# Hybrid decoder block on one core: rows of x loaded first, small products regrouped in shared breaks, the convolution's chains set apart, fh at another address

## The chip, the cores and the metric

One NeuronCore of a Trainium2 chip runs the whole block in one launch. The metric is device time in microseconds (us), lower is better. A run's time is somewhat longer than the span that the profile shows from the first to the last instruction of one profiled execution.

## The reference, cut to what matters

256 tokens of width 1024, one layer. Everything is float32.

```
n = rmsnorm(x, norm1_g);  z = n @ w_in        # conv u, conv gate, q, k, v, two branch gates
a = u * sigmoid(gate)
y_conv = silu(layernorm(depthwise_conv31(a))) @ w_conv_out
att = attention(rmsnorm(q), rmsnorm(k), v)    # 8 heads of 128, ALiBi, causal; one block of 256
merged = sigmoid(gc) * y_conv + sigmoid(ga) * (att @ w_attn_out)
h = x + merged @ w_out
out = h + (silu(n2 @ w_gate) * (n2 @ w_up)) @ w_down      # n2 = rmsnorm(h, norm2_g), width 2816
```

## The kernel before, in words

**Main products.** Each weight and each activation is split into a high and a low fp32r part, and a product is three matmuls per k-tile: high by high (L141), low activation by high weight (L142), high activation by low weight (L143). The stationary operand is 128 tokens of the activation, the moving one 512 columns of weights. The work is cut into 147 *slots*; a slot is one 512-KB piece of weights (two k-tiles by 512 columns) and issues 12 matmuls: six for token tile 0, six for token tile 1. The slots are, in order: conv (slots 0 to 15), q0 k0 v0 (16 to 27), q1 k1 v1 (28 to 39), g, ao, co, wo, gu and, last, dn, whose activations are the tiles fh and fl. SyncE (SP) streams the raw pieces; ScalarE (ACT) makes `whi` of each (L123), VectorE (DVE) or, for every second piece of slots 12 to 59, GpSimd (POOL) makes `wlo` (L124), six slots ahead.

**The order of the rest.** Four lists of jobs per slot are emitted in program order by the loop at L663 to L696: `pre` ahead of the slot, `jobs` between its two token tiles, `post` behind its second tile, `late` after that. Every engine runs its own queue in that order, so an instruction that waits holds all that stands behind it on its engine. A place in a slot where TensorE (PE) leaves the main matmuls for small ones is called a *break* here.

**Start.** Eight k-rows of x (`xt`, each 256 tokens and one float of gain) come in five DMAs between the first pieces of weights; ACT and DVE split them into `xgh` and `xgl`. POOL adds the squares of x (L631, L633), and in slot 4 PE sums them over the partitions with a column of ones (`ss`, L648).

**Depthwise convolution.** Its 248 taps run on DVE (L219 first tap of a tile, L221 the others), 31 per tile of 128 channels, as two chains: even tiles in PSUM buffer cv0, odd tiles in cv1. When a tile is done, DVE clears the head of its buffer (`clear`, L203), and REFILL slots later PE transposes the next tile into it (`refill`, L209). `run_taps` (L224) deals the taps out over the slots by a planner's costs (SLOT, TAP, LAG) and alternates between the chains. A finished pair of tiles is transposed back for the layer norm (`norm_stats`, L284).

**Heads.** Of each group of four heads, `turn` (L375) transposes q and k (`tq`, read by ACT into qT and kT, L380, L381), `score` (L383, `sc`) multiplies them, DVE adds the bias and takes the maximum (L394), ACT takes the exponentials and divides (L402, L408), `turn_p` (`tp`, L413) transposes, `values` (`pv`, L421) multiplies by v. Their PSUM tiles all come from the tag `tr` with two buffers. The tiles q and k of a group have one buffer each (`scale`, L338): the scaled q of heads 4 to 7 is written over that of heads 0 to 3.

Of the kernel before, what the change touches and what calls it, by code (L numbers as in the profile page):

```python
# [16 lines left out]
P = 128  # L17
# [24 lines left out]
AHEAD = 6  # L42
# slots after which the next heads follow
HEAD_STEP = ((0, 3, 6, 9), (0, 3, 5, 7))
# weights of the work, by which the taps are dealt out over the slots
SLOT = 2.6
# [3 lines left out]
LAG = 1.0  # L50
REFILL = 2
WARM = 8
TABLE_SLOT = 57


class Chunk:
    """CW output columns of one product, for all tokens: nk k-tiles in pieces of G."""

# [6 lines left out]
def hybrid_block(ctx: ExitStack, tc: tile.TileContext, x, xT, par, w_in, w_co, w_ao, w_o, w_gu, w_dn, out):  # L65
# [13 lines left out]

# [1 line left out]
    slots = []  # L81
# [4 lines left out]
    def add(*chunks):  # L86
        """One chunk, or two of which each half is done in turn."""
        n = chunks[0].nk // G
        parts = [range(n)] if len(chunks) == 1 else [range(n // 2), range(n // 2, n)]
        for part in parts:  # L90
            for c in chunks:
                slots.extend((c, g) for g in part)
# [7 lines left out]
    def stream_dma(upto):  # L100
        while at["dma"] < min(upto, len(slots)):
            i = at["dma"]
            c, g = slots[i]
            raw[i] = wp.tile([P, G, CW], F32, tag="raw", bufs=RAW_BUFS, name=f"raw{i}")
            for part in parts(i):
                nc.sync.dma_start(raw[i][:, part, :], c.w[g][:, part, :])
                between(i, part)
            at["dma"] += 1
# [24 lines left out]
    def mm3(c, i, g, t, acc=None, cols=slice(0, CW), first=0, last=None):  # L133
        """Piece g of the chunk for token tile t; the sum runs from k-tile first to last."""
        xh, xl = c.lhs()
        acc = c.acc[t] if acc is None else acc
        last = c.nk - 1 if last is None else last
        tok = slice(t * P, (t + 1) * P)
        for j in range(G):
            k = g * G + j  # L140
            nc.tensor.matmul(acc, xh[:, k, tok], hi[i][:, j, cols], start=(k == first), stop=False)  # L141
            nc.tensor.matmul(acc, xl[:, k, tok], hi[i][:, j, cols], start=False, stop=False)  # L142
            nc.tensor.matmul(acc, xh[:, k, tok], lo[i][:, j, cols], start=False, stop=(k == last))  # L143

# [1 line left out]
    prm = cst.tile([P, N_PAR], F32, name="prm")  # L146
    xt = ea.tile([P, KD, S + 1], F32, tag="vs", name="xt")
    xs = cst.tile([P, T, D], F32, name="xs")

# [1 line left out]
    warm = cst.tile([P, CW], BF16, name="warm")  # L151
    nc.vector.memset(warm, 0.0)
# [5 lines left out]
    load_table(AF.Sigmoid)  # L158
    wps = bank("wps", CW)
    for _ in range(WARM):  # L160
        nc.tensor.matmul(wps, warm[:, :P], warm, start=True, stop=True)
    ident = cst.tile([P, P], F32, name="ident")
    make_identity(nc, ident)
    mhalf = cst.tile([P, 8], F32, name="mhalf")
    nc.gpsimd.memset(mhalf, -0.5)
# [10 lines left out]
    def rsqrt_mean(o, ss, n, width):  # L176
        """o = (ss / n + EPS) ** -0.5"""
        nc.gpsimd.tensor_scalar(o, ss, 1.0 / n, EPS, op0=ALU.mult, op1=ALU.add)
        nc.gpsimd.tensor_tensor(o, o, mhalf[:, :width], op=ALU.pow)

# [1 line left out]
    xg, aoT, yT, mT, hT = {}, {}, {}, {}, {}  # L182
# [7 lines left out]

# [1 line left out]
    cacc, ca = {}, {}  # L192
# [12 lines left out]
    def refill(ch):  # L205
        """The channels of the next tile go on the partitions, after KC - 1 zeros."""
        j, cv = ch["next"], ch["cv"]
        for t in range(T):
            nc.tensor.transpose(cv[:, KC - 1 + t * P : KC - 1 + (t + 1) * P],  # L209
                                ca[j // 2][:, t, (j % 2) * P : (j % 2 + 1) * P], ident)  # L210
        cacc[j] = ea.tile([P, S], F32, tag="cacc", bufs=4, name=f"cacc{j}")
        ch["j"], ch["k"], ch["next"] = j, 0, j + 2
# [11 lines left out]
    def run_taps(slot, until):  # L224
        while load["dve"] + TAP <= until:
            live = [ch for ch in chains if ch["j"] is not None]
            if not live:
                return
            load["turn"] += 1
            ch = live[load["turn"] % len(live)]  # L230
            conv_tap(ch)
            load["dve"] += TAP if len(live) > 1 else TAP_ALONE
            if ch["k"] == KC:
                j, ch["j"] = ch["j"], None
                want_refill(slot, ch)
                if j % 2:
                    last = j == KD - 1
                    at_ = slot + 3
                    while not last and busy[at_] > 1:
                        at_ += 1  # L240
                    busy[at_] += 1
                    jobs[at_].append(lambda p=j // 2: norm_stats(p))
                    pe_side[at_] += 0.45
                    dve_side[at_] += 0.7
                    if last:
                        for i in range(4):
                            (post if i % 2 else jobs)[at_ + 2 + i // 2].append(lambda i=i: norm_back(2 * i))

    def want_refill(slot, ch):
        j = ch["next"]  # L250
        if j < KD and j // 2 in ca:
            clear(ch)
            slot += REFILL
            post[slot].append(lambda: refill(ch))
            pe_side[slot] += 0.25
            dve_side[slot] += 0.1
# [58 lines left out]

# [1 line left out]
    vs = {}  # L317
# [36 lines left out]
    def v_done(b):  # L354
        def done(slot, acc):
# [5 lines left out]
            late[slot + 1].append(lambda: evac(0))  # L361
            late[slot + 2].append(lambda: evac(1))
            for i in range(4):
                head(slot + 1 + i, slot + 2 + HEAD_STEP[b][i], 4 * b + i)
        return done

    def head(first, slot, h):
        hs = slice((h % 4) * P, (h % 4 + 1) * P)
# [14 lines left out]
        def score():  # L383
            s["bias"] = sm.tile([P, 3, P], F32, tag="bias", name=f"bias{h}")
            nc.scalar.mul(s["bias"], dist, 2.0 ** (-8.0 * (h + 1) / H))
            s["sc"] = bank(f"sc{h}", 4, P)
            nc.tensor.matmul(s["sc"][:, 0, :], s["q"][:, :P], s["k"][:, :P], start=True, stop=True)
            nc.tensor.matmul(s["sc"][:, 1:3, :], s["q"][:, P:], s["k"], start=True, stop=True)
            most()
# [35 lines left out]

        for i in (first, slot, slot + 4, slot + 5):
            busy[i] += 1
        pe_side[first] += 0.45
        pe_side[slot] += 0.65
        pe_side[slot + 4] += 0.35  # L430
        pe_side[slot + 5] += 0.65
        dve_side[slot] += 0.7
        dve_side[slot + 5] += 0.35
        jobs[first].append(turn)
        jobs[slot].append(score)
        pre[slot + 2].append(expo)
        pre[slot + 3].append(divide)
        jobs[slot + 4].append(turn_p)
        jobs[slot + 5].append(values)

# [1 line left out]
    sgs = ea.tile([P, 2, T, D], F32, tag="sgs", name="sgs")  # L442
# [21 lines left out]

# [1 line left out]
    def merge_done(b):  # L466
# [26 lines left out]

# [1 line left out]
    s2 = sm.tile([P, T, 2], F32, bufs=1, name="s2")  # L495

# [37 lines left out]

# [1 line left out]
    ff = {}  # L536
# [42 lines left out]

# [1 line left out]
    for p in range(KD // 2):  # L581
# [18 lines left out]

# [1 line left out]
    xg[0] = pair("xg")  # L602

    def load_x(k0, k1):
        nc.sync.dma_start(xt[:, k0:k1, :], xT[:, k0:k1, :])

    def between(i, part):
        if i == 0:
            load_x(part.start, part.stop)
            if part.stop == G:  # L610
# [4 lines left out]
    def split_x(k):  # L615
        g = xt[:, k, S:]
        nc.scalar.activation(xg[0][0][:, k, :], xt[:, k, :S], AF.Copy, scale=g)
        nc.vector.scalar_tensor_tensor(xg[0][1][:, k, :], xt[:, k, :S], g, xg[0][0][:, k, :].bitcast(F32),
                                       op0=ALU.mult, op1=ALU.subtract)
# [4 lines left out]
    def square(q):  # L624
        """Squares of x, summed over the parts of its rows that share a partition."""
        if q == 0:
            nc.scalar.activation(sq, xt[:, :2, :S], AF.Square)
            return
        s = sm.tile([P, 2, S], F32, tag="u", name=f"xsq{q}")
        nc.scalar.activation(s, xt[:, 2 * q : 2 * q + 2, :S], AF.Square)  # L630
        nc.gpsimd.tensor_add(sq, sq, s)  # L631
# [3 lines left out]
    for i in range(6):  # L635
# [4 lines left out]
        if i >= 2:  # L640
            square(i - 2)
    ones = cst.tile([P, 1], F32, name="ones")
    nc.gpsimd.memset(ones, 1.0)

    def first_norm():
# [12 lines left out]

# [1 line left out]
    n = len(slots)  # L660
# [85 lines left out]
```

## Time and profile before

| what | value |
|---|---|
| median of 3 runs | 446.02 us (445.62 to 446.30) |
| span of the profiled execution, first to last instruction | 443.5 us |
| median less span | 2.5 us |
| PE busy | 437.6 us, 99% |
| DVE, ACT, POOL busy | 309.6, 243.9, 87.5 us |
| clock granted to PE | full in all 40 slices |

No time is given for the profiled execution itself beside its span; the 2.5 us between span and median lie ahead of the first and behind the last instruction. A row of a timeline has the start, the length, the engine, the line, the operation with output and inputs, how many instructions follow each other, and in brackets the engine's idle time before it with what ended it. Matmuls overlap: what one costs on PE is the distance to the next start, not its length.

### The profile page before, as it was taken

What the parts mean: (1) busy time and instruction counts of PE and PEld (TensorE: products, weight loads), DVE (VectorE), ACT (ScalarE), POOL (GpSimd) and SP (SyncE); (2) the same over time, 40 slices, a digit from 0 to 9 for tenths busy, and PEclk for the clock granted to TensorE, in tenths of its full rate; (3) what the DMA queues carried; (4) which work ended last, traced back from release to release, by engine and by line L of the source; (5) the groups of instructions that cost most, each with busy time, mean ns of one, the idle gap of its engine ahead of it and who ended that gap; (6) DMA issues with size and microseconds to landing.
All of it is one profiled execution on the core that took longest, in us unless ns stands there. A gap on an engine that the chain in (4) does not pass through costs nothing.

```text
span 443.5 us, 5743 instructions
## 1 busy us (share of the span) xinstructions
PE 437.6 (99%) x2026; PEld 359.6 (81%) x2026; DVE 309.6 (70%) x523; ACT 243.9 (55%) x439; POOL 87.5 (20%) x73
## 2 busy tenths in 40 slices
PE   8999999999999999999999999999999999999997
PEld 4788888888888888888888888888888888888886
DVE  5989999898899799967586575555555555644501
ACT  6854466689998676639325374444444444633200
POOL 1614465745462443100000000000000000000000
PEclk9999999999999999999999999999999999999999
DMA  8986684355345444544837337655555555585001
GB/s 274 345 271 213 211 303 150 144 185 197 142 149 185 142 137 150 190 163 161 293 95 247 133 120 253 196 189 184 184 185 179 187 181 184 184 252 204 25 0 49
DMA packets 23340, 80.21 MB, mean 181 GB/s; under 512 B 2576, under 2 KB 3216, under 8 KB 23312
## 3 DMA queue, kind: packets, MB, share of 16 engines
q1 hardware_dynamic: 22896, 78.66, 52.9%
q10 hardware_dynamic: 416, 1.19, 0.8%
q8 instruction: 16, 0.26, 0.3%
q14 instruction: 12, 0.10, 0.1%
HBM read 78.79 MB, written 1.05 MB: 180 GB/s over the span
## 4 chain that ended last, share of the span: by engine, by line
PE 94%; POOL 2%; ACT 2%; DMA 1%; SPq 0%; issue 0%; DVE 0%
PE gu L141 9%; PE gu L143 9%; PE gu L142 9%; PE dn L141 4%; PE dn L143 4%; PE dn L142 4%; PE g L143 3%; PE g L142 3%; PE g L141 3%; PE conv L141 2%; PE conv L143 2%; PE conv L142 2%; PE k L143 2%; PE v L143 2%; PE q L143 2%; PE q L141 2%
## 5 line engine op out<-in xcount | busy, mean ns | idle before, releaser
L124 DVE TENSOR_TENSOR wlo<-raw,whi 128x1024 fp32r<-128x1024 f32 (+1 forms) x125 | 153.0, 1256 | 30.5 <-ACT whi L123 29.6
L123 ACT CAST whi<-raw 128x1024 fp32r<-128x1024 f32 (+1 forms) x149 | 148.9, 1035 | 34.9 <-PE dn L142 19.8
L221 DVE SCALAR_TENSOR_TENSOR cacc<-cv,prm,cacc 128x256 f32<-128x256 f32 x240 | 97.2, 475 | 0.2
L141 PE MATMUL gu<-whi,hh 128*128 128x512 f32 x176 | 69.6, 395 | 0.0
L124 POOL TENSOR_TENSOR wlo<-raw,whi 128x1024 fp32r<-128x1024 f32 x24 | 58.1, 2426 | 54.5 <-ACT whi L123 49.6
L143 PE MATMUL gu<-wlo,hh 128*128 128x512 f32 x176 | 68.7, 390 | 0.0
L142 PE MATMUL gu<-whi,hl 128*128 128x512 f32 x176 | 68.5, 389 | 0.0
L143 PEld LDWEIGHTS gu<-wlo,hh 128*128 128x128 f32 x176 | 33.0, 188 | 7.1
L142 PEld LDWEIGHTS gu<-whi,hl 128*128 128x128 f32 x176 | 33.1, 188 | 6.6
L141 PEld LDWEIGHTS gu<-whi,hh 128*128 128x128 f32 x176 | 33.1, 188 | 6.4
L141 PE MATMUL dn<-whi,fh 128*128 128x512 f32 x82 | 32.5, 396 | 0.0
L143 PE MATMUL dn<-wlo,fh 128*128 128x512 f32 x82 | 32.4, 396 | 0.0
L142 PE MATMUL dn<-whi,fl 128*128 128x512 f32 x82 | 32.4, 396 | 0.0
L546 ACT ACTIVATE fs<-gu,rstd 128x256 f32<-128x256 f32 x22 | 10.4, 475 | 39.1 <-PE gu L143 39.1
L548 DVE SCALAR_TENSOR_TENSOR f<-gu,rstd,fs 128x256 f32<-128x256 f32 x22 | 10.6, 484 | 29.1 <-ACT fs L546 29.1
L141 PE MATMUL conv<-whi,xgh 128*128 128x512 f32 x64 | 26.1, 409 | 0.9 <-ACT whi L123 0.8
L141 PE MATMUL g<-whi,xgh 128*128 128x512 f32 x64 | 26.6, 415 | 0.0
L142 PE MATMUL conv<-whi,xgl 128*128 128x512 f32 x64 | 25.4, 398 | 0.0
L143 PE MATMUL conv<-wlo,xgh 128*128 128x512 f32 x64 | 25.4, 397 | 0.0
L143 PE MATMUL g<-wlo,xgh 128*128 128x512 f32 x64 | 25.2, 394 | 0.0
L142 PE MATMUL g<-whi,xgl 128*128 128x512 f32 x64 | 25.0, 391 | 0.0
L561 ACT CAST fh<-ftr 128x512 fp32r<-128x512 f32 x11 | 6.5, 587 | 23.9 <-PE ftr L560 23.9
(159 smaller groups left out, 746.4 us busy)
## 6 DMA issues: line engine op xcount, KB each, us to landing
raw<-in_w_in SPq DMA_DIRECT2D x53, 512.0 KB, 4.2
raw<-in_w_gu SPq DMA_DIRECT2D x44, 512.0 KB, 4.3
raw<-in_w_dn SPq DMA_DIRECT2D x22, 512.0 KB, 4.1
raw<-in_w_ao SPq DMA_DIRECT2D x8, 512.0 KB, 3.3
raw<-in_w_co SPq DMA_DIRECT2D x8, 512.0 KB, 3.3
raw<-in_w_o SPq DMA_DIRECT2D x8, 512.0 KB, 5.1
raw<-in_w_in SPq DMA_DIRECT2D x6, 256.0 KB, 4.7
xs<-in_x ACTq DMA_DIRECT2D x1, 1024.0 KB, 4.7
```

Source lines behind the costliest of these rows:

```text
L123: nc.scalar.copy(hi[i][:, part, :], r[:, part, :])
L124: eng.tensor_sub(lo[i][:, part, :], r[:, part, :], hi[i][:, part, :].bitcast(F32))
L141: nc.tensor.matmul(acc, xh[:, k, tok], hi[i][:, j, cols], start=(k == first), stop=False)
L142: nc.tensor.matmul(acc, xl[:, k, tok], hi[i][:, j, cols], start=False, stop=False)
L143: nc.tensor.matmul(acc, xh[:, k, tok], lo[i][:, j, cols], start=False, stop=(k == last))
L221: nc.vector.scalar_tensor_tensor(cacc[j], src, w, cacc[j], op0=ALU.mult, op1=ALU.add)
L546: nc.scalar.activation(sg, acc[t][:, :256], AF.Silu, scale=r)
L548: nc.vector.scalar_tensor_tensor(f[t], acc[t][:, 256:], r, sg, op0=ALU.mult, op1=ALU.mult)
L561: nc.scalar.copy(fh[:, k2, :], tr)
```

## The change

The gains move to 16 floats in front of x in `xt`, so that each row of x is 256 floats long and starts at an even place; a part of x is issued to the DMA queue ahead of the piece of weights that needs it. The warming matmuls use a 128-wide tile, and there are seven of them. The column of ones is set earlier on POOL. Both groups of heads follow each other at the distances 0, 3, 6, 9 slots; a head's `turn` goes to the slot of the head before's `score`, its `values` to the slot of the head after's `turn_p`, so that two small products share a break. REFILL is 1; a refill goes between the token tiles when that place has a break already; the even chain gets two of three taps until it leads the odd one by 12 taps, after which each chain is refilled at a time of its own; `norm_stats` joins the odd chain's refill where it can. `s2` is padded to 32 floats; it lies ahead of the tiles fh and fl in SBUF, and fh moves from byte 175136 to 174464 of a partition, fl from 197664 to 196992 (before, 32 bytes past a multiple of 64; after, on one). Comments are dropped; line numbers of the changed kernel differ by 5 to 19.

```diff
--- before.py
+++ after.py
@@ -40,21 +40,24 @@
 AHEAD = 6
-HEAD_STEP = ((0, 3, 6, 9), (0, 3, 5, 7))
+HEAD_STEP = (0, 3, 6, 9)
 SLOT = 2.6
...
 LAG = 1.0
-REFILL = 2
-WARM = 8
+REFILL = 1
+LEAD = 12
+WARM = 7
+XG = 16
 TABLE_SLOT = 57
@@ -103,6 +106,8 @@
             for part in parts(i):
+                if i == 0:
+                    load_x(part.start, part.stop)
                 nc.sync.dma_start(raw[i][:, part, :], c.w[g][:, part, :])
@@ -142,13 +147,13 @@
     prm = cst.tile([P, N_PAR], F32, name="prm")
-    xt = ea.tile([P, KD, S + 1], F32, tag="vs", name="xt")
+    xt = ea.tile([P, XG + KD * S], F32, tag="vs", name="xt")
     xs = cst.tile([P, T, D], F32, name="xs")
 
-    warm = cst.tile([P, CW], BF16, name="warm")
+    warm = cst.tile([P, P], BF16, name="warm")
     nc.vector.memset(warm, 0.0)
@@ -156,11 +161,13 @@
     load_table(AF.Sigmoid)
-    wps = bank("wps", CW)
+    wps = bank("wps", 4, P)
     for _ in range(WARM):
-        nc.tensor.matmul(wps, warm[:, :P], warm, start=True, stop=True)
+        nc.tensor.matmul(wps, warm, warm[:, None, :].to_broadcast([P, 4, P]), start=True, stop=True)
     ident = cst.tile([P, P], F32, name="ident")
     make_identity(nc, ident)
+    ones = cst.tile([P, 1], F32, name="ones")
+    nc.gpsimd.memset(ones, 1.0)
     mhalf = cst.tile([P, 8], F32, name="mhalf")
@@ -228,6 +235,11 @@
             ch = live[load["turn"] % len(live)]
+            if len(live) > 1 and load["turn"] % 3 == 0:
+                a, b = chains
+                lead = (a["j"] - b["j"] + 1) // 2 * KC + a["k"] - b["k"]
+                aim = 0 if a["j"] == KD - 2 else LEAD
+                ch = a if lead < aim else b if lead > aim else ch
             conv_tap(ch)
@@ -236,22 +248,24 @@
                     at_ = slot + 3
+                    if not last and not busy[slot + REFILL]:
+                        at_ = slot + REFILL
                     while not last and busy[at_] > 1:
                         at_ += 1
-                    busy[at_] += 1
-                    jobs[at_].append(lambda p=j // 2: norm_stats(p))
+                    (post if at_ == slot + REFILL else jobs)[at_].append(lambda p=j // 2: norm_stats(p))
+                    busy[at_] += at_ != slot + REFILL
                     pe_side[at_] += 0.45
...
                         for i in range(4):
-                            (post if i % 2 else jobs)[at_ + 2 + i // 2].append(lambda i=i: norm_back(2 * i))
+                            jobs[at_ + 2 + i // 2].append(lambda i=i: norm_back(2 * i))
 
...
             slot += REFILL
-            post[slot].append(lambda: refill(ch))
+            (jobs if busy[slot] else post)[slot].append(lambda: refill(ch))
             pe_side[slot] += 0.25
@@ -360,11 +374,15 @@
             late[slot + 2].append(lambda: evac(1))
+            at_ = [slot + 2 + i for i in HEAD_STEP]
             for i in range(4):
-                head(slot + 1 + i, slot + 2 + HEAD_STEP[b][i], 4 * b + i)
-        return done
-    def head(first, slot, h):
+                head(at_[i - 1] if i else slot + 1, at_[i], at_[i + 1] + 4 if i < 3 else at_[i] + 5, 4 * b + i)
+        return done
+    def head(first, slot, end, h):
         hs = slice((h % 4) * P, (h % 4 + 1) * P)
@@ -384,8 +402,8 @@
             s["sc"] = bank(f"sc{h}", 4, P)
+            nc.tensor.matmul(s["sc"][:, 1:3, :], s["q"][:, P:], s["k"], start=True, stop=True)
             nc.tensor.matmul(s["sc"][:, 0, :], s["q"][:, :P], s["k"][:, :P], start=True, stop=True)
-            nc.tensor.matmul(s["sc"][:, 1:3, :], s["q"][:, P:], s["k"], start=True, stop=True)
             most()
@@ -423,22 +441,22 @@
 
-        for i in (first, slot, slot + 4, slot + 5):
+        for i in (first, slot, slot + 4, end):
             busy[i] += 1
...
         pe_side[slot + 4] += 0.35
-        pe_side[slot + 5] += 0.65
+        pe_side[end] += 0.65
         dve_side[slot] += 0.7
-        dve_side[slot + 5] += 0.35
+        dve_side[end] += 0.35
+        jobs[slot].insert(0, score)
         jobs[first].append(turn)
-        jobs[slot].append(score)
         pre[slot + 2].append(expo)
...
         jobs[slot + 4].append(turn_p)
-        jobs[slot + 5].append(values)
+        jobs[end].append(values)
     sgs = ea.tile([P, 2, T, D], F32, tag="sgs", name="sgs")
@@ -491,8 +509,8 @@
 
-    s2 = sm.tile([P, T, 2], F32, bufs=1, name="s2")
+    s2 = sm.tile([P, 32], F32, bufs=1, name="s2")[:, : 2 * T].rearrange("p (t b) -> p t b", b=2)
 
@@ -598,36 +616,39 @@
 
+    def xk(k0, k1):
+        return xt[:, XG + k0 * S : XG + k1 * S].rearrange("p (k s) -> p k s", s=S)
     def load_x(k0, k1):
-        nc.sync.dma_start(xt[:, k0:k1, :], xT[:, k0:k1, :])
+        cols = slice(XG + k0 * S if k0 else 0, XG + k1 * S)
+        nc.sync.dma_start(xt[:, cols], xT[:, cols])
 
...
         if i == 0:
-            load_x(part.start, part.stop)
             if part.stop == G:
...
     def split_x(k):
-        g = xt[:, k, S:]
-        nc.scalar.activation(xg[0][0][:, k, :], xt[:, k, :S], AF.Copy, scale=g)
-        nc.vector.scalar_tensor_tensor(xg[0][1][:, k, :], xt[:, k, :S], g, xg[0][0][:, k, :].bitcast(F32),
+        g, one = xt[:, k : k + 1], slice(k, k + 1)
+        nc.scalar.activation(xg[0][0][:, one, :], xk(k, k + 1), AF.Copy, scale=g)
+        nc.vector.scalar_tensor_tensor(xg[0][1][:, one, :], xk(k, k + 1), g, xg[0][0][:, one, :].bitcast(F32),
                                        op0=ALU.mult, op1=ALU.subtract)
...
         if q == 0:
-            nc.scalar.activation(sq, xt[:, :2, :S], AF.Square)
+            nc.scalar.activation(sq, xk(0, 2), AF.Square)
             return
         s = sm.tile([P, 2, S], F32, tag="u", name=f"xsq{q}")
-        nc.scalar.activation(s, xt[:, 2 * q : 2 * q + 2, :S], AF.Square)
+        nc.scalar.activation(s, xk(2 * q, 2 * q + 2), AF.Square)
         nc.gpsimd.tensor_add(sq, sq, s)
@@ -639,9 +660,6 @@
             square(i - 2)
-    ones = cst.tile([P, 1], F32, name="ones")
-    nc.gpsimd.memset(ones, 1.0)
     def first_norm():
@@ -723,7 +741,8 @@
         "x": x,
-        "xT": np.concatenate([x.T, i["norm1_g"].reshape(D, 1)], axis=1).reshape(KD, P, S + 1).transpose(1, 0, 2),
+        "xT": np.concatenate([vec(i["norm1_g"]), np.zeros((P, XG - KD), np.float32),
+                              x.T.reshape(KD, P, S).transpose(1, 0, 2).reshape(P, KD * S)], axis=1),
         "par": par,
...
         "w_co": cols(i["w_conv_out"][0]),
```

**DVE, the first tile of the even chain (slots 17 to 19).** Here `cacc_368` and `cacc_371` are the first tiles of the even and odd chain in the kernel before, `cacc_367` and `cacc_370` in the changed one; `cv_...` are the PSUM buffers that are cleared. Before:

```order
L221 SCALAR_TENSOR_TENSOR cacc_371<-cv_316,prm,cacc_371 128x256 [waits DVE_49]
L221 SCALAR_TENSOR_TENSOR cacc_368<-cv_314,prm,cacc_368 128x256 [waits DVE_49]
L221 SCALAR_TENSOR_TENSOR cacc_371<-cv_316,prm,cacc_371 128x256 [waits DVE_49]
L203 MEMSET cv_683 128x30 [waits DVE_49]
L221 SCALAR_TENSOR_TENSOR cacc_368<-cv_314,prm,cacc_368 128x256
L203 MEMSET cv_686 128x30 [waits DVE_49]
L124 TENSOR_TENSOR wlo_726<-raw_600,whi_725 128x1024 [waits DMAHW4_49,PE_49,Activation_49]
L219 TENSOR_SCALAR cacc_737<-cv_683,prm 128x256 [waits PE_49]
```

Now:

```order
L228 SCALAR_TENSOR_TENSOR cacc_367<-cv_313,prm,cacc_367 128x256 [waits DVE_49]
L228 SCALAR_TENSOR_TENSOR cacc_370<-cv_315,prm,cacc_370 128x256 [waits DVE_49]
L228 SCALAR_TENSOR_TENSOR cacc_367<-cv_313,prm,cacc_367 128x256 [waits DVE_49]
L210 MEMSET cv_635 128x30 [waits DVE_49]
L228 SCALAR_TENSOR_TENSOR cacc_370<-cv_315,prm,cacc_370 128x256
L228 SCALAR_TENSOR_TENSOR cacc_370<-cv_315,prm,cacc_370 128x256 [waits DVE_49] x2
L226 TENSOR_SCALAR cacc_660<-cv_635,prm 128x256 [waits PE_49]
L228 SCALAR_TENSOR_TENSOR cacc_370<-cv_315,prm,cacc_370 128x256 [waits DVE_49]
```

The first clear moves from behind the 61st tap to behind the 50th, and taps of one chain now stand next to each other (the `x2` row; nine such neighbours ahead of this clear).

**PE, the first refill.** Before, both chains are refilled between the slots 21 and 22 (k). Now the even one is refilled between the slots 18 and 19 (q), the first row of the piece being the last matmul of slot 18. Before:

```order
L143 MATMUL k_1_689<-wlo_603,xgh 128x512
L209 MATMUL cv_683<-ident,ca_387 128x128 [waits DVE_49]
L209 MATMUL cv_683<-ident,ca_387 128x128
L209 MATMUL cv_686<-ident,ca_387 128x128 [waits DVE_49]
L209 MATMUL cv_686<-ident,ca_387 128x128
L141 MATMUL k_0_688<-whi_623,xgh 128x512 [waits Activation_49]
L142 MATMUL k_0_688<-whi_623,xgl 128x512
```

Now:

```order
L147 MATMUL q_1_592<-whi_521,xgl 128x512
L148 MATMUL q_1_592<-wlo_522,xgh 128x512
L216 MATMUL cv_635<-ident,ca_386 128x128 [waits DVE_49]
L216 MATMUL cv_635<-ident,ca_386 128x128
L146 MATMUL q_0_591<-whi_546,xgh 128x512 [waits Activation_49]
L147 MATMUL q_0_591<-whi_546,xgl 128x512
```

The refill of the even chain moves three slots forward on PE, that of the odd one goes behind slot 22.

**ACT, the slots 34 to 36.** `q_1220` (`q_1233` before) is the scaled q of heads 4 to 7, `tq_1254` the transposed q and k of head 3. Before:

```order
L285 COPY yt<-ytr_1219 128x2x256 [waits PE_49]
L344 ACTIVATE q_1233<-q_0_951,m 128x128 [waits Pool_49]
L344 ACTIVATE q_1233<-q_0_951,m 128x128 x3
L408 ACTIVATE p_1195<-p_1195,den_1196 128x128 [waits Pool_49]
L408 ACTIVATE p_1195<-p_1195,den_1196 128x256 [waits Activation_49]
L344 ACTIVATE q_1233<-q_1_952,m 128x128 x4
L123 CAST whi_1255<-raw_1036 128x1024 [waits DMAHW2_49]
L385 ACTIVATE bias_1259<-dist 128x384
L123 CAST whi_1289<-raw_1073 128x1024 [waits DMAHW3_49]
```

Now:

```order
L358 ACTIVATE q_1220<-q_0_953,m 128x128 [waits PE_49,Pool_49]
L358 ACTIVATE q_1220<-q_0_953,m 128x128 x3
L426 ACTIVATE p_1186<-p_1186,den_1187 128x128 [waits Pool_49]
L426 ACTIVATE p_1186<-p_1186,den_1187 128x256 [waits Activation_49]
L358 ACTIVATE q_1220<-q_1_954,m 128x128 x4
L128 CAST whi_1242<-raw_1039 128x1024 [waits DMAHW2_49]
L403 ACTIVATE bias_1246<-dist 128x384
L398 ACTIVATE qT_1259<-tq_1254,gqs 128x256 [waits PE_49]
L399 ACTIVATE kT_1260<-tq_1254,prm 128x256
```

The first scaling of q has a new wait on PE, and head 3's qT and kT stand behind it.

**PE, the middles of the slots 35 and 36.** Now, in slot 35:

```order
L405 MATMUL sc_1248<-kT_1118,qT_1117 128x256 [waits Activation_49]
L406 MATMUL sc_1248<-kT_1118,qT_1117 128x128
L395 MATMUL tq_1254<-ident,q_791 128x128 [waits DVE_49,Activation_49]
L395 MATMUL tq_1254<-ident,q_791 128x128
L395 MATMUL tq_1254<-ident,k_916 128x128 x2
```

and twelve main matmuls later, in slot 36:

```order
L148 MATMUL v_0_1276<-wlo_1072,xgh 128x512
L439 MATMUL pv_1292<-pT_1156,vs 128x256 [waits PE_49,Activation_49]
L440 MATMUL pv_1292<-pT_1156,vs 128x128
L431 MATMUL tp_1297<-ident,p_1186 128x128 [waits DVE_49]
L431 MATMUL tp_1297<-ident,p_1186 128x128 x2
```

The wait on PE in ACT's rows above is for the transposes of `q_791`, the q of heads 0 to 3; the wait of `pv` on ACT is for `kT_1260`, the last reader of `tq_1254`, whose PSUM buffer `pv` takes; that of `tp` on DVE is for the maximum over `sc_1248`. Before, head 3's `turn` stood in slot 31, and `sc` alone in the break of slot 35.

## Rows read from the trace of the kernel before

**Rows 1.** The page: busy time of each engine, its share of the span, instructions.

```profile
PE 437.6 (99%) x2026; PEld 359.6 (81%) x2026; DVE 309.6 (70%) x523; ACT 243.9 (55%) x439; POOL 87.5 (20%) x73
```

**Rows 2.** Windows: each engine's busy time and count, PEclk, DMA share, GB/s.

```profile
50.00:70.00 20.00, 20.00 (x92) 16.56 (x91) 19.46 (x43) 10.57 (x25) 10.65 (x8) 1.00 0.77 266
```

**Rows 3.** Timeline of PE in dn, whose start-to-start distances are even between them.

```profile
400.10 0.40 PE L141 MATMUL dn<-whi,fh 128*128 128x512 f32 x1
...
403.60 0.40 PE L141 MATMUL dn<-whi,fh 128*128 128x512 f32 x1
```

**Rows 4.** Timeline of PE in gu, a stretch without a break.

```profile
330.02 0.39 PE L142 MATMUL gu<-whi,hl 128*128 128x512 f32 x1
...
333.19 0.39 PE L141 MATMUL gu<-whi,hh 128*128 128x512 f32 x1
```

**Rows 5.** The page's costliest groups: the matmuls of dn, first line of three.

```profile
L141 PE MATMUL dn<-whi,fh 128*128 128x512 f32 x82 | 32.5, 396 | 0.0
```

**Rows 6.** Timeline of PE around one break (the refill of both chains).

```profile
69.30 0.60 PE L209 MATMUL cv<-ident,ca 128*128 128x128 f32 x4
69.66 0.48 PE L141 MATMUL k<-whi,xgh 128*128 128x512 f32 x1
69.97 0.40 PE L142 MATMUL k<-whi,xgl 128*128 128x512 f32 x1
```

**Rows 7.** Timeline of POOL at the start: the sums of squares.

```profile
20.32 1.60 POOL L633 TENSOR_TENSOR sq<-sq 128x256 f32<-128x256 f32 x1
21.87 0.09 POOL L643 MEMSET ones<- 128x1 f32 x1
```

**Rows 8.** Timeline of PE around the sum over the partitions.

```profile
21.09 0.39 PE L143 MATMUL conv<-wlo,xgh 128*128 128x512 f32 x1
22.01 0.61 PE L648 MATMUL ss<-ones,sq 128*128 128x1 f32 x4 [0.53 <-POOL ones L643]
```

**Rows 9.** Timeline of DVE ahead of the first refill.

```profile
60.74 4.00 DVE L221 SCALAR_TENSOR_TENSOR cacc<-cv,prm,cacc 128x256 f32<-128x256 f32 x10
64.66 1.21 DVE L124 TENSOR_TENSOR wlo<-raw,whi 128x1024 fp32r<-128x1024 f32 x1
65.80 2.17 DVE L221 SCALAR_TENSOR_TENSOR cacc<-cv,prm,cacc 128x256 f32<-128x256 f32 x5
67.53 0.61 DVE L203 MEMSET cv<- 128x30 f32 x2
```

**Rows 10.** Timeline of PE: the first matmul of slot 19.

```profile
61.14 0.39 PE L141 MATMUL q<-whi,xgh 128*128 128x512 f32 x1
```

**Rows 11.** Timeline of ACT from the first scaling of q on (slots 34, 35).

```profile
110.14 1.15 ACT L344 ACTIVATE q<-q,m 128x128 f32<-128x128 f32 x4
...
113.77 0.59 ACT L385 ACTIVATE bias<-dist 128x384 f32<-128x384 f32 x1
114.20 1.10 ACT L123 CAST whi<-raw 128x1024 fp32r<-128x1024 f32 x1
```

**Rows 12.** Groups by line: kT on ACT (busy, mean ns, idle before).

```profile
L381 ACT ACTIVATE kT<-tq,prm 128x256 f32<-128x256 f32 x8 | 3.7, 467 | 0.0
```

**Rows 13.** Timeline of PE around `sc` in the middle of slot 35.

```profile
112.21 0.38 PE L387 MATMUL sc<-kT,qT 128*128 128x128 f32 x2
...
112.68 0.58 PE L141 MATMUL k<-whi,xgh 128*128 128x512 f32 x1
```

**Rows 14.** Timeline of PE: one head's `turn`.

```profile
98.19 0.38 PE L377 MATMUL tq<-ident,q 128*128 128x128 f32 x2
98.41 0.38 PE L377 MATMUL tq<-ident,k 128*128 128x128 f32 x2
98.55 0.47 PE L141 MATMUL q<-whi,xgh 128*128 128x512 f32 x1
```

**Rows 15.** Timeline of PE in the first slot.

```profile
7.95 0.63 PE L142 MATMUL conv<-whi,xgl 128*128 128x512 f32 x1
8.38 0.63 PE L143 MATMUL conv<-wlo,xgh 128*128 128x512 f32 x1
```

## The prediction, made before the changed kernel had run

> **What bounds the kernel now.** I read the page first: PE is busy for 99% of the span [rows 1], so the time is what PE's queue takes, and the change can gain only where PE spends less per product or has fewer stops, and lose only where PE stops. PE has stops before 22 us alone: waits for the first loads, and one for POOL's sum. Next the windows: from 50 to 70 us DVE is busy 19.46 of 20.00 us beside a full PE [rows 2], so there DVE has no room, and whatever makes PE wait for DVE costs time; ACT with 10.57 us has room on average, which says nothing of its order. Then I compared distances between main matmuls in two stretches without breaks: in dn 15 distances take 3.50 us, 0.2333 each [rows 3]; in gu 14 take 3.17 us, 0.2264 [rows 4]. Last I looked at DVE, ACT and PE around the places where the order moves.
>
> **Gains, each worked out.**
> *fh at another address.* dn has 82 matmuls on each of three lines [rows 5], 246 in all, with the same shapes as gu. The visible difference of dn's operands is that fh and fl start 32 bytes past a multiple of 64. If that is the cause, dn comes to 0.2264, and 246 x 0.0069 = 1.7 us go; the 36 half-wide ones at the end add about 0.1. Bounds: 0 (address has no part) and 1.8. I take 1.8, since no other difference shows.
> *Shared breaks.* PE leaves the main products 45 instead of 52 times; all small matmuls remain. Four transposes cost 0.36 to the next start, and the matmul behind them 0.31 instead of 0.226 [rows 4, 6]: a break costs some 0.04 beyond its own products when the slow matmul is shared. 7 x 0.04 = 0.3 us, bounds 0.1 and 0.7 (all of the 0.08 and a little of what follows).
> *Start.* The sum over the partitions begins at 22.01, when POOL has written the sum (20.32 + 1.60) and then the ones [rows 7, 8]; PE's last main matmul had begun at 21.09. Earlier x shortens PE's waits ahead of this place, but POOL's sum comes no earlier unless ACT's squares do; so what PE gains there it waits again. The ones set earlier give 0.1. Bounds 0 and 1.0. Even addresses of x: nothing, ACT and DVE are not late in what they split there, and at the start only the landings count.
> The padding of s2, the wider moving operand of the warming and the order of the halves of `sc` cost nothing: they lie in idle time or keep the same columns.
> Gains together: 1.8 + 0.3 + 0.1 = 2.2 us.
>
> **Costs, each worked out.**
> *First refill of the even chain.* It now stands ahead of slot 19 and waits for a clear that follows the 50th tap. Before, ten taps start at 60.74, 0.392 apart, and then, behind a low part, five, the last of them behind the first clear [rows 9]; that is, the ten are numbers 48 to 57, and the 50th starts at 61.53 and ends at 62.0. A clear takes 0.3: 62.3. PE reaches slot 19 at 61.14 [rows 10]. That alone is 1.2 us. In the new order nine neighbours ahead of it are of one chain. The row that has such a dependence is the clear at 67.53 behind the tap that starts at 65.80 + 3 x 0.392 = 66.98: 0.55 instead of 0.39 [rows 9]. That includes a change of operation, so I take 0.1 per neighbour, bounds 0 and 0.16: 0.9 us (0 to 1.4). DVE and PE have the same work ahead of this place as before, apart from that. Cost 2.1 (1.2 to 2.6).
> *Refill of the odd chain*, ahead of slot 23. From clear to clear DVE has 23 taps (9.0), two low parts of at least 1.2 [rows 9], three neighbours (0.3) and a clear (0.3): 12.0. PE has four slots of 12 x 0.2264 = 2.72 and one refill (0.2): 11.1. Cost 0.9 (0.4 to 1.6, since low parts that meet POOL's take longer).
> *Third and fourth refill*, ahead of the slots 31 and 35: by the same sum the third has room, the fourth lacks 0.4 (0 to 1.0).
> *Head 3's turn in slot 35.* The first scaling of q for heads 4 to 7 now waits on PE for it. `sc` begins at 112.21 and takes 0.47 [rows 13], `turn` another 0.36 [rows 14]; so ACT starts the scaling at about 113.0, not at 110.14 [rows 11], when its last q transpose has been written, and PE goes on at 113.05. Ahead of kT3 stand eight scalings, two divisions, a high part and a bias: 114.20 - 110.14 = 4.06 [rows 11]; then qT and kT, 0.4 to 0.47 each [rows 12]: 4.9 us. PE has twelve main matmuls, 2.72, and a recovery of 0.1 until `pv`, which waits for kT3. Cost 4.9 - 2.8 = 2.1 (1.5 to 2.6). All of it comes onto PE, whenever PE arrives there, since ACT's chain starts with PE's own transposes.
> *Last refill*, middle of slot 44: 15 taps with seven neighbours, one low part and others since the clear before, some 9 us against two slots and breaks of PE, some 7; what DVE made up during the stop in slot 36 covers most. Cost 0.7 (0 to 1.8).
> Other new waits (`tp`, `tq` of later heads, `norm_back`) have 0.6 us or more of room, worked out in the same way.
> Costs together: 2.1 + 0.9 + 0.4 + 2.1 + 0.7 = 6.2 us.
>
> **Sum.** 443.5 - 2.2 + 6.2 = 447.5 us of span; with the 2.5 us around it, which the change doesn't touch, 450.0 us. The sum goes from one profiled execution to the median of the runs by that difference.
>
> **Rivals.**
> *The stops don't come (faster).* Both groups of stops hang on a few handovers: if DVE's clear comes before 61.1 us and ACT drains in time for `pv`, PE never stops, and 2.2 us of gain stay: 443.8 us. For it: DVE's lag behind PE is set by what PE and POOL hand it, and gaps that a trace of one order shows need not be there in another. Against it: 62.3 against 61.14, and 4.9 against 2.8, are not close. It decides in favour if DVE's backlog at slot 18 is under 2 us and kT3 ready within 2.8 us of the turn.
> *dn stays at 0.2333.* Then the padding has done nothing and 1.8 us are missing: 451.8 us. For it: no row of before shows one product at both addresses. The Trainium skill, page "TensorE: Matmul & The Clock Gate", section on where the extra 2.5 ns come from, gives the distance of back-to-back matmuls by columns and clock alone, 215.7 ns for 512 columns, so by it dn and gu would be alike and no address would matter. The trace disagrees: neither 0.2264 nor 0.2333 is that, and two equal shapes differ by 3%, so something that the rule lacks is at work.
> *The neighbours of one chain are free.* Then the first refill costs 1.2, the second 0.6, the fourth and the last 0.1 and 0.4; with 2.1 for slot 36 that is 4.4: 448.2 us. It is inside my forecast's own range.
> *The clock falls in a stop.* In the first slot matmuls are 0.43 apart [rows 15] against 0.226 later; PE had worked with long waits until then. A stop of 2.1 us with others around it might bring that spacing back for some 4 us: eight matmuls at 0.2 more, 1.7 us: 451.7. Against it: the stop of 0.5 to 0.9 us at 21 to 22 us [rows 8] left 0.23 behind it. The same page of the Trainium skill, in its table of the two states, has an idle engine fall back to half clock; no run here shows a stop long enough.
> *x first brings the sum of squares forward by 1.0 us*: 449.0.
>
> **How the numbers follow.** A run of this kernel can tell 0.2%, 0.9 us, from no change. My forecast with both versions of the neighbours and the earlier sum, 447.5 to 451: 0.68, all slower. dn unchanged or a fallen clock: 0.10, slower. No stops at all: 0.12, faster. Half of the stops, sum near zero: 0.10, no change (445.1 to 446.9). So faster 0.12, same 0.10, slower 0.78. The range leaves out the stop-free case and the dearest: 445.5 to 452.0. Likeliest, 450.0.
>
> **What would show it.** Right: PE waits of about 2 us for the clear ahead of slot 19 and for ACT's kT ahead of `pv` near 118 us, smaller ones ahead of the slots 23 and 44; ACT idle for about 3 us ahead of the first scaling of q; dn at 0.226 to 0.227. Wrong: no wait of PE behind 22 us, or a wait of DVE for PE at the refill; dn still at 0.2333; spacings of 0.43 behind a stop.

## The result, and the profile after

| | before | changed |
|---|---|---|
| median of 4 runs each, side by side | 446.16 us | 450.78 us |
| span of the profiled execution | 443.5 us | 448.4 us |

The change is slower: ratio 1.0107, 95% interval 1.0086 to 1.0128. The forecast was 450.0 us. The page of the changed kernel, against [rows 1], has PE's work unchanged and a longer span:

```profile
span 448.4 us, 5734 instructions
PE 437.7 (98%) x2025; PEld 360.2 (80%) x2025; DVE 310.5 (69%) x523; ACT 244.7 (55%) x439; POOL 88.5 (20%) x73
```

Its waits of PE (engine, line, releaser: total, times, longest) name two that the kernel before did not have, `pv` and `cv`; the third, at the start, was 0.53 us there [rows 8]:

```profile
PE pv L439 <- ACT kT L399: 2.1, 1, 2.1
PE cv L216 <- DVE cv L210: 1.8, 2, 1.3
PE ss L666 <- POOL sq L654: 1.3, 1, 1.3
```

The timeline of PE shows what each stop costs, as the distance from the start of the last main matmul to the start of the product that waited, less the usual 0.227: 1.47 us ahead of slot 19, 0.67 ahead of slot 23, 2.28 in slot 36.

```profile
61.30 0.39 PE L148 MATMUL q<-wlo,xgh 128*128 128x512 f32 x1
62.99 0.44 PE L216 MATMUL cv<-ident,ca 128*128 128x128 f32 x2 [1.31 <-DVE cv L210]
...
73.95 0.39 PE L148 MATMUL k<-wlo,xgh 128*128 128x512 f32 x1
74.85 0.44 PE L216 MATMUL cv<-ident,ca 128*128 128x128 f32 x2 [0.51 <-DVE cv L210]
...
114.72 0.47 PE L146 MATMUL k<-whi,xgh 128*128 128x512 f32 x1
...
117.34 0.39 PE L148 MATMUL v<-wlo,xgh 128*128 128x512 f32 x1
119.85 0.70 PE L439 MATMUL pv<-pT,vs 128*128 128x256 f32 x2 [2.13 <-ACT kT L399]
```

Together these are 4.42 of the 4.9 us that the span grew. The start added 0.36 (slot 5 begins at 22.84, before at 22.48), a short wait at the last refill some 0.3, and dn gave back 0.24.

ACT in slots 35 and 36 is the chain of [rows 11] put behind PE. It sits idle until the transposes of q are done, then needs 4.95 us to the end of kT (114.85 to 119.80):

```profile
114.85 1.14 ACT L358 ACTIVATE q<-q,m 128x128 f32<-128x128 f32 x4 [1.73 <-PE tq L395]
115.86 0.81 ACT L426 ACTIVATE p<-p,den 128x128 f32<-128x128 f32 x2
116.56 1.16 ACT L358 ACTIVATE q<-q,m 128x128 f32<-128x128 f32 x4
117.56 1.09 ACT L128 CAST whi<-raw 128x1024 fp32r<-128x1024 f32 x1
118.49 0.58 ACT L403 ACTIVATE bias<-dist 128x384 f32<-128x384 f32 x1
118.92 0.52 ACT L398 ACTIVATE qT<-tq,gqs 128x256 f32<-128x256 f32 x1
119.27 0.53 ACT L399 ACTIVATE kT<-tq,prm 128x256 f32<-128x256 f32 x1
```

In dn 14 distances take 3.25 us, 0.232 each. In [rows 3] it is 0.2333, and the forecast was 0.2264:

```profile
402.82 0.39 PE L148 MATMUL dn<-wlo,fh 128*128 128x512 f32 x1
...
406.07 0.39 PE L147 MATMUL dn<-whi,fl 128*128 128x512 f32 x1
```

### The profile page after: what moved, and what is told of

It reads as the page before. It is cut to its first block, busy times and chain, and to the rows that moved or that the text cites. A ratio compares the mean times of both kernels' runs of the same rounds, so it can differ in the third digit from the quotient of the medians.

```text
span 448.4 us, 5734 instructions
## 1 busy us (share of the span) xinstructions
PE 437.7 (98%) x2025; PEld 360.2 (80%) x2025; DVE 310.5 (69%) x523; ACT 244.7 (55%) x439; POOL 88.5 (20%) x73
## 4 chain that ended last, share of the span: by engine, by line
PE 79%; DVE 13%; ACT 2%; DMA 2%; issue 1%; SPq 1%; POOL 0%; DVEq 0%; ACTq 0%
PE gu L148 9%; PE gu L146 9%; PE gu L147 9%; DVE cacc L228 8%; DVE wlo L129 4%; PE dn L146 4%; PE dn L148 4%; PE dn L147 4%; PE g L148 3%; PE g L146 3%; PE g L147 3%; PE ao L148 2%; PE ao L146 2%; PE wo L148 2%; PE co L148 2%; PE wo L146 2%
## 5 line engine op out<-in xcount | busy, mean ns | idle before, releaser
L228 DVE SCALAR_TENSOR_TENSOR cacc<-cv,prm,cacc 128x256 f32<-128x256 f32 x240 | 100.1, 475 | 1.3
L129 POOL TENSOR_TENSOR wlo<-raw,whi 128x1024 fp32r<-128x1024 f32 x24 | 59.8, 2495 | 56.7 <-ACT whi L128 56.7
```

The costliest lines, as they stand in the source:

```text
L129: eng.tensor_sub(lo[i][:, part, :], r[:, part, :], hi[i][:, part, :].bitcast(F32))
L228: nc.vector.scalar_tensor_tensor(cacc[j], src, w, cacc[j], op0=ALU.mult, op1=ALU.add)
```

## The experiments

### The two handovers, undone one at a time and together

`e1`: head 3's turn goes back to slot 31.

```diff
-                head(at_[i - 1] if i else slot + 1, at_[i], ...
+                head(slot + 4 if (b, i) == (0, 3) else at_[i - 1] if i else slot + 1, at_[i], ...
```

> The changed kernel with one thing undone: the turn of head 3 goes back from slot 35 to slot 31. Theory (a handover through the one buffer of q): ACT no longer waits for PE ahead of the scaling of q, the stop of 2.3 us ahead of pv in slot 36 goes, and the time falls from 450.8 by about 2.3, to 448.5 us; the stops ahead of the two refills stay as they are. Rival (DVE is late there anyway): the stop only changes its name, to a wait of tp or pv for DVE's maximum, and the time falls by less than 1 us.

Measured: 448.63 us, ratio to before 1.0053 (1.0034 to 1.0072). The wait for kT is gone. A smaller one, which the long stop had covered, stands in its place, so part of the rival holds too: `tp` waits for DVE's maximum, 1.12 us from the start of the last `pv` product. In the changed kernel, where the long stop came first, that distance is 0.11, so the wait costs 1.0.

```profile
118.77 0.38 PE L440 MATMUL pv<-pT,vs 128*128 128x128 f32 x2
120.00 0.52 PE L431 MATMUL tp<-ident,p 128*128 128x128 f32 x3 [0.85 <-DVE nmx L412]
```

By the traces the stops shrink by 2.28 - 1.0 = 1.3 us, and from slot 5 to the end the profiled execution is 1.6 us shorter (423.9 against 425.5). By the medians the time falls by 2.15, and the two intervals allow all of these.

`e2`: the chains as before.

```diff
-REFILL = 1
+REFILL = 2
-            if len(live) > 1 and load["turn"] % 3 == 0:
...
-                ch = a if lead < aim else b if lead > aim else ch
...
-                    if not last and not busy[slot + REFILL]:
-                        at_ = slot + REFILL
...
-            (jobs if busy[slot] else post)[slot].append(lambda: refill(ch))
+            post[slot].append(lambda: refill(ch))
```

> The changed kernel with the chains as before (alternating taps, both refilled together two slots later); heads, start and padding stay changed. Theory (only the new place of the refill makes PE wait): the stops of 1.5 and 0.7 us ahead of the slots 19 and 23 go with their recoveries, 2.3 us in all: 448.5 us, with the stop ahead of pv still there. Rival (DVE is the bound in these slots): the stops come back at the old places of the refills, and the time stays above 450 us.

Measured: 449.65 us, ratio 1.0072 (1.0048 to 1.0096), with runs from 447.4 to 451.7. No `cv` wait is left in the trace and the one for kT stays, as the theory has it; the median is 1.2 us above it. The spread of the ten executions goes with TensorE's granted clock: the three at 1.00 took 447.4 to 448.0 us, the three at 0.995 to 0.996 took 449.1 to 449.7, and the four at 0.992 took 450.6 to 451.7. So at full clock the time is below the theory's 448.5, and the median is raised by the executions with a lower one. The profiled execution (450.55 us, 0.992) shows two falls. The first follows the wait for POOL's sum at the start; in the window behind it (the last three figures are PEclk, DMA share, GB/s) the granted clock is 0.61 on average, and matmuls are 0.43 apart.

```profile
PE ss L659 <- POOL sq L647: 1.4, 1, 1.4
22.00:26.00 4.00, 3.90 (x13) 3.15 (x14) 3.47 (x4) 0.20 (x1) 0.50 (x2) 0.61 0.77 199
```

The second follows the stop in slot 36. There the granted clock is 0.60 and 0.54, and matmuls are 0.42 apart:

```profile
118.00:120.00 2.00, 1.64 (x6) 1.46 (x6) 2.00 (x8) 1.24 (x2) 0.68 (x1) 0.60 0.29 82
120.00:122.00 2.00, 2.00 (x7) 1.67 (x7) 2.00 (x7) 1.70 (x8) 1.70 (x1) 0.54 0.47 180
122.00:124.00 2.00, 2.00 (x11) 1.63 (x10) 2.00 (x6) 2.00 (x9) 0.50 (x1) 1.00 0.62 186
```

```profile
118.36 1.20 PE L432 MATMUL pv<-pT,vs 128*128 128x256 f32 x2 [2.09 <-ACT kT L392]
...
120.86 0.63 PE L147 MATMUL v<-whi,xgl 128*128 128x512 f32 x1
121.28 0.63 PE L148 MATMUL v<-wlo,xgh 128*128 128x512 f32 x1
```

So PE fell from 2.4 to 1.2 GHz after it had stood for 1.4 us, and again after 2.1 us. In the changed kernel's own profiled execution stops of 1.3 and 2.1 us, the waits of `ss` and `pv` above, left the next matmuls at 0.23. Whether a stop of this size is followed by the lower clock differs between executions; what decides it is not shown.

`e12`: both edits.

> Both things undone at once. Theory (independent handovers): 450.8 - 2.3 - 2.3 = 446.2 us, what is left against the kernel before being the later start (+0.4) and dn (-0.2). Rival (the stops cover for each other): one of them comes back elsewhere, 447.5 us or more.

Measured: 446.71 us, ratio 1.0005 (0.9987 to 1.0023): no different from before. Neither stop comes back elsewhere, and the `tp` wait of e1 is gone too. Behind the start one short wait is left that the kernel before did not have, that of the last `norm_stats` for DVE's last tap:

```profile
PE ytr L291 <- DVE cacc L228: 0.4, 1, 0.4
```

### The start alone

The edits to `xt`, `load_x`, `ones`, `warm` on the kernel before.

> The kernel before with the start of the change alone (layout of x, x ahead of the weights, ones earlier, warming). Theory (more waits of ACT for loads make the sum of squares later): PE's sum over the partitions starts about 0.4 us later than before, 22.4 us, and the time is 446.5 us. Rival (the later landings of the changed kernel's profile were chance): the sum is at 22.0 us or earlier, and the time 446.0 us or less.

Measured: 445.87 us, ratio 0.9989 (0.9973 to 1.0005). In its profile the sum did start late, at 22.65, as the theory has it, but the time did not move, as the rival has it. In the profiles of the three kernels below whose start is that of before and whose s2 alone is padded, POOL's sum ended at 22.18, 22.43 and 22.54; before, at 21.92; in the changed kernel, at 22.32. So the 0.36 us of the changed kernel lie within what one start differs from execution to execution: neither gain nor loss is shown.

### The address of fh

The kernel before with s2 padded to 32, 64 or 128 floats, which moves fh and fl and nothing that PE reads ahead of them.

```diff
-    s2 = sm.tile([P, T, 2], F32, bufs=1, name="s2")
+    s2 = sm.tile([P, 64], F32, bufs=1, name="s2")[:, : 2 * T].rearrange("p (t b) -> p t b", b=2)
```

> The kernel before with s2 padded to 32 floats alone (the change's own padding): fh starts at byte 175232 of a partition, 128 past a multiple of 256 (and on a multiple of 64, as in the changed kernel). Theory A (the spacing of dn depends on the address of fh, but on a coarser grid than 64 bytes): dn at about 0.2325 as in the changed kernel, the time falls by 0.2, 445.7 us. Theory B (multiples of 64 bytes are enough and something else in the changed kernel spoilt it): dn at 0.2267, 444.3 us. Theory C (the address has no part, the values of fh or the length of the sum do it): 0.2333, 445.9 us.

> The same with 64 floats: fh starts at 175360, a multiple of 256 but not of 512. Theory A with a grid of 256 bytes: dn at 0.2267, 444.3 us; with a grid of 512: slower than that, between 0.228 and 0.233. Theory C: 0.2333 and 445.9 us.

> The same with 128 floats: fh starts at 175616, a multiple of 512. Theory A: dn at 0.2267, 246 x 0.0066 = 1.6 us less, 444.3 us. Theory C: 0.2333 and 445.9 us.

| start byte of fh | bytes past a multiple of 256 | dn, us apart | median us | ratio to before |
|---|---|---|---|---|
| 175136 (before) | 32 | 0.2333 | 445.88 | 1 |
| 175232 | 128 | 0.232 | 445.35 | 0.9985 (0.9975 to 0.9995) |
| 175360 | 0 | 0.2267 | 443.99 | 0.9955 (0.9939 to 0.9970) |
| 175616 | 0 (and of 512) | 0.2267 | 444.17 | 0.9964 (0.9948 to 0.9979) |

Timeline of dn with 175360, 15 distances in 3.40 us:

```profile
399.74 0.39 PE L141 MATMUL dn<-whi,fh 128*128 128x512 f32 x1
...
403.14 0.39 PE L141 MATMUL dn<-whi,fh 128*128 128x512 f32 x1
```

So far a grid of 256 bytes fits, and one of 64 or 512 does not. The addresses are worked out from the sizes of the tiles, since the traces do not hold them; the steps of 96, 224 and 480 bytes follow from the edits alone. The version with 64 floats beats both kernels, 444.0 us.

The changed kernel with both handovers undone and fh on that grid:

> The changed kernel with the turn of head 3 and the chains undone (as in the run of both at once), and fh moved on by 128 bytes to a multiple of 512 (174592). Theory A: dn at 0.2267, 1.4 us less than the 446.7 of that kernel: 445.3 us. Theory C: 446.7 us.

Measured: 445.22 us, ratio 0.9978 (0.9967 to 0.9990): the gain of dn carries over. The shared breaks add none that shows: this kernel is 1.2 us slower than the kernel before with the same padding (443.99), and by the traces the stop at the last `norm_stats` costs 0.6 of that, by the distance of the starts, and a later start 0.4. It is no test of all seven breaks saved, since with the chains undone it has only two breaks fewer than the kernel before.

Next, which operand counts. On the kernel before, gap tiles of 128 bytes in the pool of the weights move the stationary operands of conv to gu off the grid (fh stays on it), or the moving ones alone, or, third, all of both. s2 is padded in each so that fh lies where this wants it. The gap of the first:

```diff
             hi[i] = wp.tile([P, G, CW], F32R, tag="whi", bufs=SPL_BUFS, name=f"whi{i}")
             lo[i] = wp.tile([P, G, CW], F32R, tag="wlo", bufs=SPL_BUFS, name=f"wlo{i}")
+            if i == 0:
+                nc.gpsimd.memset(wp.tile([P, 32], F32, name="gap0"), 0.0)
```

> The kernel before with fh and fl on a multiple of 256 bytes (175360), and the stationary operands of all other main products moved 128 bytes off that grid (xgh, hh and so on from 115200 to 115328). Theory (the stationary operand's place on a grid of 256 bytes sets the distance, whatever its values and the length of the sum): dn stays at 0.2267, and conv to gu, about 1480 matmuls, go to about 0.2325: some 1480 x 0.0058 = 8 us more than 444.0, 450 to 453 us, less where breaks interrupt the pattern. Rival (only dn, with its long sums, is open to it): conv to gu stay at 0.2267 and the time at 444.0 us.

> The kernel before with all stationary operands on multiples of 256 bytes, and the moving ones (whi, wlo) 128 bytes off. Theory 1 (the stationary operand alone counts, as its loads are what stands between the matmuls): 0.2267 everywhere, 444.0 us. Theory 2 (any operand that PE reads counts, or their distance from each other does): about 0.2325 everywhere, 1770 x 0.0058 = 10 us more, about 454 us.

> The kernel before with every operand of the main products 128 bytes past a multiple of 256: the stationary ones (115328, fh 175488) and the moving ones (49792 and on). Theory 1 (each operand has to lie on the grid by itself): 0.232 or more everywhere, the dn stretch included, 453 us or more. Theory 2 (only the distance between the two operands counts, modulo 256): 0.2267 everywhere and 444.0 us.

Measured: 451.72 (ratio 1.0126, 1.0069 to 1.0183), 452.37 (1.0141, 1.0089 to 1.0193) and 444.58 us (0.9963, 0.9934 to 0.9991). Fifteen distances of conv, in the timelines of the first, the second and the third: 3.49, 3.48 and 3.40 us.

```profile
41.69 0.40 PE L145 MATMUL conv<-wlo,xgh 128*128 128x512 f32 x1
...
45.18 0.40 PE L145 MATMUL conv<-wlo,xgh 128*128 128x512 f32 x1
```

```profile
41.79 0.39 PE L147 MATMUL conv<-wlo,xgh 128*128 128x512 f32 x1
...
45.27 0.39 PE L147 MATMUL conv<-wlo,xgh 128*128 128x512 f32 x1
```

```profile
41.87 0.39 PE L145 MATMUL conv<-wlo,xgh 128*128 128x512 f32 x1
...
45.27 0.39 PE L145 MATMUL conv<-wlo,xgh 128*128 128x512 f32 x1
```

The products of dn fit: with fh on the grid they are 0.227 us apart in the first kernel, where whi and wlo are on it too, and 0.2325 in the second, where these are 128 bytes off; in the third, with all 128 bytes off, 0.227. Either operand 128 bytes off slows the product, both together do not. So at the distances tried (0, 32 and 128) it is the distance between the two start addresses, modulo 256 bytes, that counts. The values in the operands and the length of the sum have no part, since the same products run at either speed. Why the distance counts is not shown.

## Why the prediction was right, and where its sum was not

The direction and the mechanism of the stops held. That the time came so near is partly luck: three errors cancel. The sum had costs of 6.2 and gains of 2.2, net 4.0; the profiled executions show +4.7 of stops, +0.36 of start and -0.24 of dn, 4.8 of the 4.9 that the span grew. So the costs were 1.5 too high, and the gains too high by 2.3. The third error is the 2.5 us between span and median, which do not lie around the span alone. In every run with its span on record the time is only about 1.8 us longer than that span (450.19 against 448.4); the other 0.7 is that the execution profiled before took about 443.5 + 1.8 = 445.3, less than any of the four behind the median of 446.16. With 1.8 the same sum gives 449.3 us for an execution that took 450.19.

*Head 3's turn: right.* 2.1 forecast, 2.28 measured, by the chain as it was added up (4.9 forecast, 4.95 found; PE's part 2.8 forecast, 2.85 found, 114.72 to 117.57). ACT was idle for 1.14 us ahead of the copy before the scaling and for 1.73 just ahead of it, 2.9 in all where some 3 were forecast.

*Refills: right in place, too dear.* First 2.1 forecast, 1.47 found; second 0.9 and 0.67; fourth 0.4 and none; last 0.7 and some 0.3. The neighbours of one chain were priced about right: the ten taps of the last row below hold two such pairs and take 4.25 us where [rows 9] has 4.00, 0.125 a pair for 0.1 forecast, so 1.1 for the nine instead of 0.9. What failed is the clause that DVE and PE have otherwise the same work ahead of this place. DVE's low parts that meet POOL's got shorter with the new order, 2.17 for 2.55 and, one later, 1.63 for 1.98, some 0.7 us in all ahead of the first clear. The rows show why. Before, the low part ends at 38.77, 1.08 us behind the end of POOL's (37.69); in the changed kernel at 39.16, again 1.08 us behind it (38.08). The other two such low parts ahead of the clear end 1.08 to 1.09 us behind POOL's as well, in both kernels. So what the neighbours add ahead of such a low part is mostly spent waiting for POOL anyway.

Before:

```profile
32.91 4.78 POOL L124 TENSOR_TENSOR wlo<-raw,whi 128x1024 fp32r<-128x1024 f32 x2 [6.15 <-ACT whi L123]
36.22 2.55 DVE L124 TENSOR_TENSOR wlo<-raw,whi 128x1024 fp32r<-128x1024 f32 x1
```

Changed:

```profile
33.30 4.78 POOL L129 TENSOR_TENSOR wlo<-raw,whi 128x1024 fp32r<-128x1024 f32 x2 [6.14 <-ACT whi L128]
36.99 2.17 DVE L129 TENSOR_TENSOR wlo<-raw,whi 128x1024 fp32r<-128x1024 f32 x1
39.08 4.25 DVE L228 SCALAR_TENSOR_TENSOR cacc<-cv,prm,cacc 128x256 f32<-128x256 f32 x10
```

*dn: wrong.* "If that is the cause, dn comes to 0.2264": an address was the cause, but not its place on 64 bytes. What counts is its distance from the moving operand's, modulo 256, and the change put fh 128 bytes past a multiple of that. The term was 1.8; the trace shows 0.24, and the run of the padding alone 0.5 by medians. The lower bound, 0, was nearer. The rival that dn stays came nearly true, for another reason than it gave. The 1.6 us that dn did not give were made up by stops that cost less than forecast and by the 0.7 us above.

*Shared breaks: too large.* 0.3 forecast, 0.04 a break. `pv` and `tp` in one break take 1.03 us beyond the main products, apart 0.68 + 0.37 (the kernels with fh on the grid, up to the twelfth main matmul behind the break); that is 0.02 to 0.03 saved per break. Two refills in breaks of their own cost 2 x 0.25 where the common one costs 0.46, and give as much back.

*Start: not shown.* -0.1 forecast, nothing that can be told from chance measured.

Of the rivals, the one without stops did not come true: with both handovers undone (e12) the stops went, but the time was 446.7 and not 443.8, since the gains of dn and of the breaks were missing. The fallen clock is not in the changed kernel's profiled execution and is in that of e2, once behind a stop of 1.4 us, shorter than the 2.1 that the rival took. It may have raised one of the four times of the changed kernel: 452.09 us with a granted clock of 0.995, where the three at 1.00 took 450.2 to 450.9; no trace covers that execution. Its price of 1.7 us was about right: the medians of e2's three groups lie 1.8 and 1.4 us apart.

## What to carry to other kernels

Before a small product is moved next to another, follow what reads its result and what overwrites its source: here one buffer of q turned a move on PE into a wait of ACT, and all that stood behind it on ACT came back to PE. Where equal matmuls run at different distances, compare the start addresses of the stationary and the moving operand modulo 256 bytes before looking for work to save; here 224 bytes of padding gave 1.9 us, and the rearrangement lost 4.6. An engine that is full for 20 us has no place for a handover that comes earlier. And before work is added up ahead of such a handover, look whether an instruction on the way waits for another engine: what is added ahead of that one may cost little, as DVE's taps did here.

## What the runs showed of the hardware

Two operands whose start addresses differ by 32 or 128 bytes modulo 256 put matmuls of 128x512 fp32r at 0.2333 and 0.232 us instead of 0.2267; over a whole kernel 128 bytes cost 8 us (452 against 444). The Trainium skill, page "SBUF — State Buffer", section "Operand start alignment", states the element's size as the condition for a start address and says that this is about legality, not speed. The runs show that speed has another condition, with the three distances above.

A stop of PE of 1.4 or 2.1 us can be followed by some 3 us at the lower clock, 0.42 to 0.43 a matmul (e2); stops of 1.3 and 2.1 us in another execution were not (the changed kernel). The Trainium skill, page "TensorE: Matmul & The Clock Gate", table of the two states, has an idle engine fall back to 1.2 GHz; the trace of e2 agrees with the fall itself.

A low part on DVE (two tiles of SBUF in, 1.21 us alone) that starts while POOL is at work on one of its own ends 1.08 to 1.09 us after POOL's, so it takes 1.63 to 2.55 us by when it starts. This holds for all six such low parts ahead of slot 19 in the two kernels.
